# A hybrid convolution and linear-attention encoder layer in fp32: Strassen-Winograd products of halves for the projections and the final product, in a phase of their own

## The chip, the core and the metric

The kernel runs on one core of one Trainium2 chip, in one launch. The metric is the device time of one execution in microseconds (us). TensorE (PE) multiplies, VectorE (DVE), ScalarE (ACT) and GpSimd (POOL) do elementwise work, SyncE (SP) and ACT issue the DMAs that move data between DRAM and the on-chip SBUF; PE writes to PSUM, here eight banks of 128 x 512 fp32. DVE and ACT read PSUM, POOL cannot.

## The reference

Two sequences s of 1024 tokens with 1024 features go through one layer. Cut to what matters:

```
h     = rmsnorm(x) * (1 + scale) + shift                 # shift, scale, gate = silu(c) @ w_ada + b_ada
a_b, a_c, a_x, a_z, q, k, v, b_z, lr_f, lr_b, m_a, m_b = split(h @ w_in)
u     = conv3(a_c * a_x) + bias                          # along the tokens, feature by feature
y_a   = (a_b * u * silu(a_z)) @ w_a_out
g_f/b = log_sigmoid(lr_f/b @ w_gate + b_gate) / 16       # decays of the linear attention
o     = attention(q, k, v, g_f, forward) + attention(q, k, v, g_b, backward)   # 4 heads
y_b   = (rmsnorm(o) * silu(b_z)) @ w_b_out
y     = rmsnorm(x + gate * ((sigmoid(m_a) * y_a + sigmoid(m_b) * y_b) @ w_out))
```

All in fp32: eleven products of 1024 x 1024 by 1024 x 1024 for a sequence (q and k are half as wide), and the attention beside them.

## The kernel before, in words

**Products.** Every operand of a dense product is split into a rounded high part and a low rest (`split`, lines 112 to 116: an ACT cast, then a DVE or POOL subtraction), and three matmuls stand for one: high by high, high by low, low by high (`product`, lines 128 to 133). One weight tile has 128 output features; `halves` multiplies it by the activations of one sequence, which lie in SBUF as `hh` and `hl`, in two halves of 512 tokens and two steps of 12 matmuls each: 48 matmuls of 128 x 512 for a tile. The values are an exception: `values` takes the activations as the stationary operand and 256 columns of weights as the moving one, 192 matmuls of 128 x 256 for a head.

**Stages.** `start` prepares the modulation and the activations of sequence 0 and multiplies the first three weight tiles as they appear. `mixers(s)` then goes through the four heads: the projections for queries, keys, values and z gates of the head, with the decays beside them on ACT and DVE, and then `attention`. The attention of a head is a chain: seven levels of block length B = 1 to 64, where DVE multiplies Q, K and T in place, ACT rearranges K to `km`, PE multiplies 16 blocks (line 553), and DVE copies them under a mask; then transposes, states of the chunks, outputs, a norm and transposes back. Each point where it yields names a number of steps (`FILL`), and so many steps of the convolution branch (`conv_tile`, `halves`) are put there, to keep PE busy while the chain waits: 28 steps for a head of sequence 0, 32 for one of sequence 1. `merge(s)` multiplies the two branches' outputs by w_a_out and w_b_out, with the products for the merge gates between, and puts the next stationary set (the activations of sequence 1, or w_out) in place of `hh` and `hl`. `final` multiplies by w_out, 16 blocks of 128 tokens, adds x, and normalizes.

**Order and buffers.** The order on each engine is set once, at build time, by a planner: it takes the instructions by their place in the program, lets an instruction that is ready go past an earlier one that is not, and gives each tile a buffer of its tag when one is free. There are 10 `big` buffers (two rows of 1024 fp32), 8 `small` ones (one row), 2 for weights, 3 for raw loads and four PSUM banks for the dense products (`psd`). On the chip each engine takes its instructions in that fixed order.

```
def product(out, terms, first=True, last=True):
    for i, ((ahi, alo), (bhi, blo)) in enumerate(terms):
        nc.tensor.matmul(out, ahi, bhi, ...)
        nc.tensor.matmul(out, ahi, blo, ...)
        nc.tensor.matmul(out, alo, bhi, ...)
```

## Time and profile before

| what | value |
|---|---|
| median of 3 runs | 2450.72 us (2449.0 to 2453.34) |
| the profiled execution's own time | 2453.73 us |
| its span, first to last instruction | 2451.6 us |
| mean granted TensorE clock | 0.994 |
| PE, DVE, ACT, POOL busy | 98%, 49%, 35%, 9% of the span |
| instructions of PE, DVE, ACT, POOL | 12233, 1412, 1276, 171 |
| DMA | 196.24 MB, mean 80 GB/s |

The profiled execution is 3.0 us above the median of the runs; span and own time differ by 2.1 us. A matmul's duration in the rows overlaps that of its neighbours, so the pace of PE is read from the starts of successive matmuls, not from their durations.

### The profile page before, as it was taken

The numbers are of one execution on the slowest core, as the hardware profiler recorded it, in microseconds if no ns is written. First come the engines' busy times: TensorE is split into PE (matmuls) and PEld (weight loads), VectorE is DVE, ScalarE is ACT, GpSimd is POOL, SyncE is SP. The second block draws the span as 40 slices with busy tenths as digits, with TensorE's granted clock in tenths as the row PEclk, the third lists the DMA queues.
The fourth block names the chain that finished last, engine by engine and source line by source line (L and its number), as shares of the span: only waits on it lengthen the run. The fifth ranks groups of instructions, "written<-read, shape, count | busy, mean of one in ns | idle before, by whom it ended". The sixth has DMA issues, their size and how long they took to land.

```text
span 2451.6 us, 28938 instructions
## 1 busy us (share of the span) xinstructions
PE 2413.9 (98%) x12233; PEld 2037.7 (83%) x12233; DVE 1210.3 (49%) x1412; ACT 851.9 (35%) x1276; POOL 229.0 (9%) x171
## 2 busy tenths in 40 slices
PE   7999999999999999999999999999999999999998
PEld 4788888888888888888888888888888888888887
DVE  6647567567367411324466466466466411323333
ACT  5443463443433311212523523524524311212221
POOL 3101001001001000011001001001001000012421
PEclk8999999999999999999999999999999999999999
DMA  6201311311211411423201201201201411324541
GB/s 248 76 26 35 112 69 52 129 69 44 69 35 44 138 52 44 129 80 135 78 31 48 78 26 52 78 26 52 78 26 52 138 44 51 129 103 137 189 137 61
DMA packets 68322, 196.24 MB, mean 80 GB/s; under 512 B 5824, under 2 KB 22816, under 8 KB 68192
## 3 DMA queue, kind: packets, MB, share of 16 engines
q1 hardware_dynamic: 60704, 167.51, 20.2%
q10 hardware_dynamic: 7488, 26.87, 2.9%
q8 instruction: 96, 1.57, 0.3%
q14 instruction: 34, 0.28, 0.0%
HBM read 159.24 MB, written 35.13 MB: 79 GB/s over the span
## 4 chain that ended last, share of the span: by engine, by line
PE 94%; DVE 3%; issue 1%; ACT 1%; DMA 1%; POOL 0%; SPq 0%; POOLq 0%; DVEq 0%; ACTq 0%
PE ps L131 28%; PE ps L133 28%; PE ps L132 28%; PE pl L553 3%; PE pm L131 2%; PE pm L132 1%; PE pm L133 1%; PE pl L170 1%; PE ps L437 1%; PE pm L684 1%; PE pm L620 0%; DVE As L115 0%; DVE w L115 0%; PE pm L218 0%; DMA araw<-in_weights_dram 0%
## 5 line engine op out<-in xcount | busy, mean ns | idle before, releaser
L131 PE MATMUL ps<-hh,w 128*128 128x512 f32 x2032 | 801.2, 394 | 4.4 <-ACT hh L189 4.4
L133 PE MATMUL ps<-hh,w 128*128 128x512 f32 x2032 | 794.2, 391 | 0.1
L132 PE MATMUL ps<-hl,w 128*128 128x512 f32 x2032 | 794.0, 391 | 0.0
L133 PEld LDWEIGHTS ps<-hh,w 128*128 128x128 f32 x2032 | 382.5, 188 | 80.9 <-DVE w L115 0.5
L131 PEld LDWEIGHTS ps<-hh,w 128*128 128x128 f32 x2032 | 383.0, 188 | 79.6 <-ACT hh L189 4.6
L132 PEld LDWEIGHTS ps<-hl,w 128*128 128x128 f32 x2032 | 383.2, 189 | 74.7
L115 DVE TENSOR_TENSOR w<-raw,w 128x1024 fp32r<-128x1024 f32 x159 | 210.8, 1326 | 271.2 <-ACT w L114 271.2
L114 ACT CAST w<-raw 128x1024 fp32r<-128x1024 f32 x159 | 166.4, 1047 | 374.0 <-PE ps L133 359.0
L131 PE MATMUL ps<-b,w 128*128 128x512 f32 x512 | 199.2, 389 | 0.0
L132 PE MATMUL ps<-b,w 128*128 128x512 f32 x512 | 199.2, 389 | 0.0
L133 PE MATMUL ps<-b,w 128*128 128x512 f32 x512 | 199.2, 389 | 0.0
L133 PE MATMUL ps<-wv,hl 128*128 128x256 f32 x512 | 144.9, 283 | 0.0
L132 PE MATMUL ps<-wv,hh 128*128 128x256 f32 x512 | 144.9, 283 | 0.0
L131 PE MATMUL ps<-wv,hh 128*128 128x256 f32 x512 | 144.9, 283 | 0.0
L457 POOL TENSOR_TENSOR u<-u,sg 128x512 f32<-128x512 f32 x32 | 45.8, 1432 | 1047.5 <-DVE sg L456 784.3
L702 ACT ACTIVATE sg<-ps 128x512 f32<-128x512 f32 x64 | 38.3, 598 | 244.5 <-PE ps L133 244.4
L131 PEld LDWEIGHTS ps<-b,w 128*128 128x128 f32 x512 | 96.1, 188 | 20.0
L132 PEld LDWEIGHTS ps<-b,w 128*128 128x128 f32 x512 | 96.1, 188 | 20.0
L133 PEld LDWEIGHTS ps<-b,w 128*128 128x128 f32 x512 | 96.1, 188 | 19.9
L726 POOL TENSOR_TENSOR sg<-m,sg 128x512 f32<-128x512 f32 x32 | 45.0, 1405 | 657.0 <-DVE sg L725 532.2
L132 PE MATMUL ps<-hl,mg 128*128 128x512 f32 (+1 forms) x264 | 101.0, 383 | 0.0
L133 PE MATMUL ps<-hh,mg 128*128 128x512 f32 (+1 forms) x264 | 101.0, 383 | 0.0
(217 smaller groups left out, 3253.6 us busy)
## 6 DMA issues: line engine op xcount, KB each, us to landing
raw<-in_weights_dram SPq DMA_DIRECT2D x184, 512.0 KB, 3.3
araw<-in_weights_dram SPq DMA_DIRECT2D x16, 512.0 KB, 4.5
ta_d<-u ACTq DMA_DIRECT2D x16, 512.0 KB, 2.7
ob_d<-sz ACTq DMA_DIRECT2D x16, 512.0 KB, 3.8
raw<-ta_d SPq DMA_DIRECT2D x16, 512.0 KB, 4.1
raw<-ob_d SPq DMA_DIRECT2D x16, 512.0 KB, 3.5
mg_d<-sg ACTq DMA_DIRECT2D x16, 512.0 KB, 3.1
raw<-mg_d SPq DMA_DIRECT2D x16, 512.0 KB, 4.2
```

Source lines behind the costliest of these rows:

```text
L114: high = nc.scalar.copy(out=hi, in_=raw)
L115: engine.tensor_sub(out=lo, in0=raw, in1=hi.bitcast(F32))
L131: nc.tensor.matmul(out, ahi, bhi, start=(first and i == 0), stop=False)
L132: nc.tensor.matmul(out, ahi, blo, start=False, stop=False)
L133: nc.tensor.matmul(out, alo, bhi, start=False, stop=(last and i == n - 1))
L170: nc.tensor.matmul(out(t), ones if x.dtype == F32R else ones.bitcast(F32), x[:, t * HALF:(t + 1) * HALF], start=(first and i == 0), stop=( ...
L437: nc.tensor.matmul(ps[:4 * RANK], w[:, k, :], h, start=(k + i == 0), stop=(k * i == KT - 1))
L457: nc.gpsimd.tensor_mul(out=u[:, sl], in0=u[:, sl], in1=sg[:, sl])
L553: nc.tensor.matmul(pl[:, j * P:(j + 1) * P], km[:, c * P:(c + 1) * P], qm(c), start=True, stop=True)
L684: nc.tensor.transpose(out=tp[:, b * P:(b + 1) * P], in_=ot[:, b, j * P:(j + 1) * P], identity=ident)
L702: run(halves(W_MA + i, lambda ps, sl: nc.scalar.activation(out=sg[:, sl], in_=ps, func=AF.Sigmoid)))
L726: nc.gpsimd.tensor_add(out=g[:, sl], in0=m1[f][:, sl], in1=g[:, sl])
```

## The change

**The seven products.** A pair of weight tiles (256 output features, 1024 inputs) is now one job. Its weights are cut into four quarters A11, A12, A21, A22 and the activations into B11 to B22 (512 inputs by 512 tokens); seven products of quarters or of sums of quarters, in the Winograd form of Strassen's method, take the place of eight. `Moving` holds the quarters and four sums of them, `stationary` makes the seven weight operands on POOL, ACT and DVE, three products ahead of PE (`AHEAD`), and `fast` runs them in three PSUM banks a, b and c: a takes products 0 and 3, c 1 and 6, b 2, 4 and 5, with the copies and DVE additions that form the four quarters of the result between them.

**What goes through it.** The convolution's products (14 jobs of sequence 0, whose first tiles still run in `start`, 16 of sequence 1), queries, keys, values and z gates (12 jobs each), in the new phase `projections`, and the final product (8 jobs): 62 jobs. Queries, keys, values, silu(z) and the decays T go to DRAM (`q_d` to `t_d`) and are loaded again by `attention`, which transposes the values on PE. The decays run beside the q, k, v and z jobs.

**The attention's fill.** `mixers` now has only the attention, with the 64 steps of the 16 merge gates spread over heads 0 to 2 and the 32 steps of the product by w_a_out over head 3, by the lengths that `LENGTHS` gives each yield. Gates and that product go to DRAM too (`g_d`, `m1_d`); `merge` has only the product by w_b_out, beside which `refill` prepares the next `Moving`; what of it is left runs after it (`run(built)`). The `hh` and `hl` tiles are gone, and there are 18 `big` buffers, of which a `Moving` takes 16, 8 of them until the projections end.

```diff
-NBIG, NSMALL, NW, NRAW = 10, 8, 2, 3
+NBIG, NSMALL, NW, NRAW = 18, 7, 4, 3
+AHEAD = 3
+LENGTHS = (8, 5, 3, 2.5, 4, 2, 2)
+LENGTH = 8 + 7 * 5 + 2 * 3 + 4 * 2.5 + 4 * 4 + 2 * 2 + 2 * 2
...
+        def sums(self, k, x):
+            t = big("t", shape=(P, 4, HALF))
+            b11, b12, b21, b22 = (x[:, r, c * HALF:(c + 1) * HALF] for r in range(2) for c in range(2))
+            nc.gpsimd.tensor_sub(out=t[:, 0, :], in0=b12, in1=b11)
+            nc.gpsimd.tensor_sub(out=t[:, 1, :], in0=b22, in1=t[:, 0, :])
+            nc.gpsimd.tensor_sub(out=t[:, 2, :], in0=b22, in1=b12)
+            nc.gpsimd.tensor_sub(out=t[:, 3, :], in0=b21, in1=t[:, 1, :])
+            return t
+        def sum_parts(self, k, t):
+            self.th[k], self.tl[k] = big("th", F32R, (P, 4, HALF)), big("tl", F32R, (P, 4, HALF))
+            for o in range(0, 4, 2):
+                split(self.th[k][:, o:o + 2, :], self.tl[k][:, o:o + 2, :], t[:, o:o + 2, :], nc.vector)
+        def quadrant_parts(self, k, x):
+            self.hi[k], self.lo[k] = big("hi", F32R), big("lo", F32R)
+            for r in range(2):
+                split(self.hi[k][:, r, :], self.lo[k][:, r, :], x[:, r, :], nc.vector)
...
+    def stationary(load):
+        def new():
+            return sb.tile([P, 2, 4 * P], F32R, name="w", tag="w", bufs=NW)
+        def parts(a):
+            t = new()
+            split(t[:, 0, :], t[:, 1, :], a, nc.vector)
+            return t
+        r1, r2 = load(0), None
+        yield None
+        r2 = load(1)
+        r1, r2 = (r.rearrange("p k c -> p (k c)") for r in (r1, r2))
+        a11, a12, a21, a22 = r1[:, :HALF], r1[:, HALF:], r2[:, :HALF], r2[:, HALF:]
+        yield parts(a11)
+        t = new()
+        x = sb.tile([P, 4 * P], F32, name="s1", tag="s1", bufs=2)
+        nc.gpsimd.tensor_add(out=x, in0=a21, in1=a22)
+        nc.scalar.copy(out=t[:, 0, :], in_=x)
+        nc.gpsimd.tensor_sub(out=a21, in0=a11, in1=a21)
+        nc.gpsimd.tensor_sub(out=a11, in0=x, in1=a11)
+        nc.vector.tensor_sub(out=t[:, 1, :], in0=x, in1=t.bitcast(F32)[:, 0, :])
+        yield t
+        yield parts(a11)
+        yield parts(a12)
+        nc.gpsimd.tensor_sub(out=a12, in0=a12, in1=a11)
+        yield parts(a21)
+        yield parts(a22)
+        yield parts(a12)
...
+    def fast(jobs, mv):
+        ops = []
+        def make():
+            later = iter(())
+            for n, (load, _, _) in enumerate(jobs):
+                gen = later if n else stationary(load)
+                if not n:
+                    next(gen)
+                for i in range(7):
+                    if i == 2 and n + 1 < len(jobs):
+                        later = stationary(jobs[n + 1][0])
+                        next(later)
+                    ops.append(next(gen))
+                    yield
+                next(gen, None)
+        maker = make()
+        for _ in range(AHEAD):
+            next(maker, None)
+        for load, place, there in jobs:
+            banks = {}
+            for i, (o, first) in enumerate(((B11, True), (0, True), (1, True), (B21, False), (2, False), (3, False),
+                                            (B22, False))):
+                next(maker, None)
+                if first:
+                    banks["acb"[i]] = dense_ps()
+                a, b, c = (banks.get(n) for n in "abc")
+                ps = banks["acbabbc"[i]]
+                w = ops.pop(0)
+                for k in range(4):
+                    (mhi, mlo), cs = mv.operand(o, k), slice(k * P, (k + 1) * P)
+                    nc.tensor.matmul(ps, w[:, 0, cs], mhi, start=(first and k == 0), stop=False, skip_group_check=True)
+                    nc.tensor.matmul(ps, w[:, 0, cs], mlo, start=False, stop=False, skip_group_check=True)
+                    nc.tensor.matmul(ps, w[:, 1, cs], mhi, start=False, stop=(k == 3), skip_group_check=True)
+                if i == 0:
+                    keep = small("keep", shape=(P, 2, HALF))
+                    p1, u2 = keep[:, 0, :], keep[:, 1, :]
+                    nc.scalar.copy(out=p1, in_=a)
+                elif i == 2:
+                    nc.vector.tensor_add(out=u2, in0=b, in1=p1)
+                elif i == 3:
+                    nc.scalar.copy(out=place(0, 0), in_=a)
+                    there(0, 0)
+                elif i == 4:
+                    d = place(1, 1)
+                    nc.vector.tensor_add(out=d, in0=b, in1=p1)
+                    nc.vector.tensor_add(out=d, in0=c, in1=d)
+                    there(1, 1)
+                elif i == 5:
+                    nc.vector.tensor_add(out=place(1, 0), in0=b, in1=p1)
+                    there(1, 0)
+                elif i == 6:
+                    nc.vector.tensor_add(out=place(0, 1), in0=c, in1=u2)
+                    there(0, 1)
+                yield
...
+    def shift(s, f, mv, x, sl):
         by = mod[:, f, 0, s:s + 1]
-        nc.scalar.activation(out=hh[:, f, sl], in_=x, func=AF.Identity, bias=by)
-        nc.vector.scalar_tensor_tensor(out=hl[:, f, sl], in0=x, scalar=by, in1=hh.bitcast(F32)[:, f, sl],
-                                       op0=ALU.add, op1=ALU.subtract)
+        hi, lo = mv.act(f, sl)
+        nc.scalar.activation(out=hi, in_=x, func=AF.Identity, bias=by)
+        nc.vector.scalar_tensor_tensor(out=lo, in0=x, scalar=by, in1=hi.bitcast(F32), op0=ALU.add, op1=ALU.subtract)
+        nc.gpsimd.tensor_scalar(out=x, in0=x, scalar1=by, scalar2=0.0, op0=ALU.add, op1=ALU.add)
...
+    def refill(mv, src, scaled):
...
+        def load(k):
+            x = big("x")
+            nc.sync.dma_start(out=x, in_=src[k::4].rearrange("b p t -> p b t"))
+            return x
+        def prepared(k, x):
             if scaled:
-                for k, x in tiles:
-                    scale(1, k, x, rr)
-            if not half:
+                for b in range(2):
+                    scale(1, k + 4 * b, x[:, b, :], rr)
+                    nc.scalar.activation(out=x[:, b, :], in_=x[:, b, :], func=AF.Identity,
+                                         bias=mod[:, k + 4 * b, 0, 1:2])
+            return mv.sums(k, x)
+        for k in range(4):
+            x = load(k)
+            yield
+            t = prepared(k, x)
+            yield
+            if k == 2:
                 yield
-            for k, x in tiles:
-                if scaled:
-                    shift(1, k, x, slice(0, L))
-                else:
-                    split(hh[:, k, :], hl[:, k, :], x, nc.vector)
+            mv.quadrant_parts(k, x)
             yield
...
+        def conv_jobs(ct):
+            pc, px, pz, pb = tile_of("big"), tile_of("big"), tile_of("small"), tile_of("small")
+            us = {}
+            def x_there(r):
+                nc.gpsimd.tensor_mul(out=row(pc, r), in0=row(pc, r), in1=row(px, r))
+                us[r] = taps(ct + r, row(pc, r))
+            def z_there(r):
+                silu(row(pz, r), row(px, r))
+                nc.gpsimd.tensor_mul(out=us[r], in0=us[r], in1=row(pz, r))
+            def b_there(r):
+                nc.vector.tensor_mul(out=us[r], in0=us[r], in1=row(pb, r))
+                nc.scalar.dma_start(out=ta_d[s][ct + r], in_=us[r])
...
+        for h in range(0, NH, 2):
+            for w, d in ((W_Q, q_d), (W_K, k_d)):
+                jobs.append(out_job(w + h, [d[s][h + r, :, 0, :] for r in range(2)]))
+            for g in range(h, h + 2):
+                jobs.append(out_job(W_V + 2 * g, [v_d[s][g, :, r, :] for r in range(2)]))
+                jobs.append(out_job(W_BZ + 2 * g, [z_d[s][g, :, r, :] for r in range(2)], True))
+        for n, _ in enumerate(fast(jobs, mv)):
+            if n + 1 >= 7 * n_conv:
+                if n + 1 == 7 * n_conv:
+                    side = chain(prepare(), gate_rows()) if s == 0 else iter(())
+                    side = chain(decays(s, mv), side)
+                next(side, None)
+        run(side)
...
+    def mixers(s, mv):
+        def gates():
+            for i in range(2 * KT):
+                sg = small("sg")
+                yield from halves(W_MA + i, lambda ps, sl: nc.scalar.activation(out=sg[:, sl], in_=ps, func=AF.Sigmoid),
+                                  mv.act)
+                nc.scalar.dma_start(out=g_d[s][i], in_=sg)
+        def first_out():
+            act = reload(ta_d[s])
+            for f in range(KT):
+                g = small("g")
+                nc.sync.dma_start(out=g, in_=g_d[s][f])
+                yield from halves(W_A + f, lambda ps, sl: nc.vector.tensor_mul(out=g[:, sl], in0=ps, in1=g[:, sl]), act)
+                nc.scalar.dma_start(out=m1_d[s][f], in_=g)
...
-                if i % 3 == 0:
-                    next(ahead, None)
-                if i % 2 == 1:
-                    next(side, None)
-            run(ahead)
-            run(side)
-            for steps in attention(s, state, h):
-                for _ in range(steps):
+            if h == NH - 1:
+                run(dense)
+                dense, each = first_out(), KT * 4.0
+                owed = 0.0
+            for length in attention(s, h):
+                owed += each * length / LENGTH
+                while owed >= 1.0:
+                    owed -= 1.0
                     next(dense, None)
...
+    def attention(s, h):
+        n_own, n_level, n_keys, n_states, n_out, n_scale, n_turn = LENGTHS
+        T, qk = big("T"), big("qk")
+        nc.sync.dma_start(out=T, in_=t_d[s][h])
         qs, kr = qk[:, 0, :], qk[:, 1, :]
+        nc.sync.dma_start(out=qs, in_=q_d[s][h, :, 0, :])
+        nc.sync.dma_start(out=kr, in_=k_d[s][h, :, 0, :])
+        nc.scalar.mul(out=qs, in_=qs, mul=float(P) ** -0.5)
...
-        V, sz = state["V", h], state["sz", h]
+        vT, sz = big("vT"), big("sz")
+        nc.sync.dma_start(out=vT, in_=v_d[s][h])
+        nc.sync.dma_start(out=sz, in_=z_d[s][h])
+        V = big("Vh", F32R, (P, TB, DV)), big("Vl", F32R, (P, TB, DV))
+        for g in range(TB // 2):
+            tp = misc_ps()
+            for b in range(2):
+                for j in range(2):
+                    nc.tensor.transpose(out=tp[:, (2 * b + j) * P:(2 * b + j + 1) * P],
+                                        in_=vT[:, j, (2 * g + b) * P:(2 * g + b + 1) * P], identity=ident)
+            gs = slice(2 * g, 2 * g + 2)
+            split(V[0][:, gs, :], V[1][:, gs, :], tp.rearrange("p (b v) -> p b v", v=DV), nc.vector)
         Td = sb.tile([P, 2, TB], F32, name="Td", bufs=2)
         nc.vector.tensor_copy(out=Td, in_=sub_ap(T, 0, [[L, 2], [P, TB]]))
...
+    def merge(s, fill):
         act = reload(ob_d[s])
         for f in range(KT):
-            g = gates[KT + f]
+            g, m1 = small("g"), small("m1")
+            nc.sync.dma_start(out=g, in_=g_d[s][KT + f])
+            nc.sync.dma_start(out=m1, in_=m1_d[s][f])
...
-            if f == KT - 5:
-                fill = refill(src, scaled)
-            if f in (KT - 5, KT - 3, KT - 2):
-                w = load_w(W_B + f + 1)
+            next(fill)
...
+            def there(r, c):
+                sl = slice(c * HALF, (c + 1) * HALF)
+                y, x, a = place(r, c), xt[r][:, sl], ss[0][:, 2 * r + c:2 * r + c + 1]
+                (nc.vector if last else nc.gpsimd).tensor_mul(out=y, in0=y, in1=gb[s][:, sl])
+                nc.vector.tensor_add(out=y, in0=y, in1=x)
+                nc.scalar.activation(out=x, in_=y, func=AF.Square, scale=float(D) ** -0.5, accum_out=a)
+                done[r] += 1
+                if done[r] < 2:
+                    return
+                q = sb.tile([P, 1], F32, name="rs", bufs=2)
+                nc.gpsimd.tensor_scalar(out=q, in0=ss[0][:, 2 * r:2 * r + 1], scalar1=ss[0][:, 2 * r + 1:2 * r + 2],
+                                        scalar2=EPS, op0=ALU.add, op1=ALU.add)
+                nc.gpsimd.tensor_tensor(out=q, in0=q, in1=mhalf[:, :1], op=ALU.pow)
+                pieces = (((0, HALF), nc.sync), ((HALF, D), nc.scalar)) if last else (((0, D), nc.sync),)
+                for (lo, hi), queue in pieces:
+                    y = ys_[0][:, r, lo:hi]
+                    nc.vector.scalar_tensor_tensor(out=y, in0=y, scalar=q, in1=fg[:, lo:hi], op0=ALU.mult, op1=ALU.mult)
+                    queue.dma_start(out=ys[s][ts[r], lo:hi], in_=y)
...
+        run(fast([job(s, i) for s in range(2) for i in range(TB // 2)], mv))
...
+    started = start(mv)
+    projections(0, mv, started)
+    mixers(0, mv)
+    mv = Moving()
+    built = refill(mv, x_t[1], True)
+    merge(0, built)
+    run(built)
+    projections(1, mv, None)
+    mixers(1, mv)
+    mv = Moving()
+    built = refill(mv, w_out.rearrange("(k p) c -> k p c", p=P), False)
+    merge(1, built)
+    run(built)
+    final(mv)
```

## Rows read from the trace of the kernel before

**Rows 1.** The page's part 1, busy time by engine.
```profile
PE 2413.9 (98%) x12233; PEld 2037.7 (83%) x12233; DVE 1210.3 (49%) x1412; ACT 851.9 (35%) x1276; POOL 229.0 (9%) x171
```

**Rows 2.** The page's part 4, the chain that ended last, by engine.
```profile
PE 94%; DVE 3%; issue 1%; ACT 1%; DMA 1%; POOL 0%; SPq 0%; POOLq 0%; DVEq 0%; ACTq 0%
```

**Rows 3.** Timeline of PE: start, duration; one weight tile, then value products.
```profile
1120.15 0.39 PE L131 MATMUL ps<-hh,w 128*128 128x512 f32 x1
...
1131.03 0.39 PE L131 MATMUL ps<-b,w 128*128 128x512 f32 x1
...
1204.96 0.28 PE L131 MATMUL ps<-wv,hh 128*128 128x256 f32 x1
...
1216.00 0.28 PE L133 MATMUL ps<-wv,hl 128*128 128x256 f32 x1
```

**Rows 4.** The chain in order of time: transposes, then level 1 of four heads.
```profile
274.11 0.87 PE pm L684 x8
...
360.59 0.93 PE pl L170 x4
...
718.92 0.93 PE pl L170 x4
...
1255.39 0.93 PE pl L170 x4
...
1809.61 0.93 PE pl L170 x4
```

**Rows 5.** Timeline of DVE, head 1 of sequence 0 (durations in us).
```profile
378.72 1.22 DVE L594 TENSOR_TENSOR Q<-Q,t 128x1024 f32<-128x1024 f32 x1
...
388.74 1.29 DVE L597 TENSOR_TENSOR K<-K,t 128x512 f32<-128x512 f32 x2
...
405.25 0.81 DVE L471 TENSOR_SCALAR u<-pr,vecs 128x1024 f32<-128x1024 f32 x1
...
408.25 1.28 DVE L474 SCALAR_TENSOR_TENSOR u<-pr,vecs,u 128x1023 f32<-128x1023 f32 x1
```

**Rows 6.** Groups of instructions by line and shape, POOL and DVE.
```profile
L726 POOL TENSOR_TENSOR sg<-m,sg 128x512 f32<-128x512 f32 x32 | 45.0, 1405 | 657.0 <-DVE sg L725 532.2 <-issue 107.4 <-DMA raw<-mg_d 17.3
L115 POOL TENSOR_TENSOR mg<-raw,mg 128x1024 fp32r<-128x1024 f32 x16 | 40.0, 2504 | 78.3 <-ACT mg L114 78.3
L770 POOL TENSOR_TENSOR rs<-ss,consts 128x1 f32<-128x1 f32 x16 | 9.0, 564 | 1.3
L767 POOL TENSOR_SCALAR ss<-ss 128x1 f32<-128x1 f32 x17 | 5.1, 302 | 48.5 <-ACT xy L764 47.5
L725 DVE TENSOR_TENSOR sg<-ps,sg 128x512 f32<-128x512 f32 x32 | 22.0, 689 | 84.1 <-PE ps L133 83.4 <-issue 0.6
L763 DVE TENSOR_TENSOR xy<-xy 128x512 f32<-128x512 f32 x31 | 21.5, 692 | 1.1
```

**Rows 7.** Timeline of POOL and of DVE, about 410 and 423 us.
```profile
410.36 4.95 POOL L115 TENSOR_TENSOR Ql<-Q,Qh 128x2048 fp32r<-128x2048 f32 x1 [116.06 <-ACT Qh L114]
...
422.94 1.29 POOL L457 TENSOR_TENSOR u<-u,sg 128x512 f32<-128x512 f32 x1 [4.45 <-DVE sg L456]
...
410.77 4.58 DVE L604 COPY Td<-t 128x16 f32<-128x16 f32 x1
...
423.10 2.21 DVE L115 TENSOR_TENSOR w<-raw,w 128x1024 fp32r<-128x1024 f32 x1
```

**Rows 8.** Issues of DMAs on SP: KB each, median us to landing.
```profile
raw<-in_weights_dram SPq DMA_DIRECT2D x36, 512.0 KB, 3.3
...
fill<-in_x_t_dram SPq DMA_DIRECT2D x4, 1024.0 KB, 6.3
```

**Rows 9.** Two stretches: us, busy us (instructions) of PE, PEld, DVE, ACT, POOL, PEclk, DMA share, GB/s.
```profile
1226.00:1371.00 145.00, 145.00 (x758) 123.65 (x758) 92.65 (x119) 51.80 (x94) 13.40 (x9) 1.00 0.16 53
...
2248.00:2451.60 203.60, 195.79 (x887) 162.93 (x885) 76.80 (x94) 45.27 (x88) 60.16 (x53) 0.99 0.39 135
```

401 lines of the change are left out of this document (200 added, 201 removed).

## The prediction

> **What bounds the kernel now.** I read the busy times first: PE is busy for 98% of the span, DVE for half of it, POOL for 9% [rows 1]. That alone would not do, since a matmul's duration overlaps the next one's; the chain that ended last says the same from the other side, 94% of it is PE [rows 2]. So a matmul less is time less, as long as nothing else takes PE's place. The pace is in the starts: a weight tile of 48 matmuls takes 1131.03 - 1120.15 = 10.88 us, 0.2267 us for each, 2.72 us for a step of 12; the value products, 256 wide, start every 0.12 us (92 between 1204.96 and 1216.00) [rows 3]. The duration column (0.39 and 0.28) would price the same work far too high.
>
> What PE waits for today is little. Level 1 of the attention comes round every (1809.61 - 1255.39) / 3 = 184.7 us in sequence 1 and (718.92 - 360.59) / 2 = 179.2 us in sequence 0 [rows 4]. A head of sequence 1 holds 32 steps (87.0), four weight tiles for q, k and z (43.5), 192 value matmuls (23.0), four decay products (0.9), which leaves 30.3 us for the attention's own matmuls, if PE never waits there; the stretch of an attention there has PE busy all through [rows 9]. The same with 28 steps (76.2) is 173.9 us, so sequence 0 idles 5.3 us a head, 21 us in all.
>
> **The change part by part.** *Removed.* 62 jobs have 84 matmuls in place of 96: 744 x 0.2267 = 168.7 us. The values become 512 wide: 1536 x 0.12 less 768 x 0.2267 is another 10.2 us. *Added on PE.* 16 transposes of values for each of eight heads, at the 0.87 us that eight transposes take [rows 4]: 128 x 0.109 = 14.0 us. The 21 us of idle time in sequence 0 go with the arrangement that made them; what comes instead is costed below. So far: 2451.6 - 168.7 - 10.2 + 14.0 - 21 = 2266 us.
>
> *DVE and POOL in a job.* A job needs 84 x 0.2267 = 19.04 us of PE. POOL makes four sums, 128 x 512, which take 1.29 us when nothing is in the way (the row at 422.94 [rows 7]; the mean of 1.405 [rows 6] holds waits). DVE makes seven low parts of 512, 0.64 us each (half of the pair at 388.74 [rows 5]), and five additions out of PSUM, 0.69 us each [rows 6]. The convolution adds, for two feature tiles (four jobs), six POOL products of 1024 (2.5 us each [rows 6]) and on DVE two sets of taps (0.81 and twice 1.28 [rows 5]) and two products of 1.22. Neither engine alone fills the 76.2 us of four jobs: POOL 35.6, DVE 40.9.
>
> But the two are not independent. A copy of 16 elements on DVE took 4.58 us: POOL had started on Q's low part 0.4 us before; a DVE subtraction of 1.22 us took 2.21 behind a POOL operation of 1.29 [rows 7]. So I add POOL's time and DVE's operations on SBUF: 35.6 + 27.1 = 63 of 76.2 us for the convolution, which leaves PE the bound. The final job is different: POOL also multiplies the four quarters by the gate and forms the norm, 8 x 1.29 + 2 x (0.30 + 0.56) = 12.0 us, DVE has 7 x 0.64 + 4 x 0.69 + 2 x 1.28 = 9.8 us on SBUF [rows 5, 6], together 21.8 against 19.04: 2.8 us short, x 8 = 22 us.
>
> The Trainium skill, page "SBUF — State Buffer", section "Who interferes with whom", has this as an exclusive lock: a DVE instruction with two SBUF inputs and a POOL instruction that reads SBUF never run together, whichever came first holds the port to its end, and a DVE instruction with one input from PSUM is free of it. Our rows show it for POOL operations that started first. By the rule the final jobs cost the 22 us; if only each engine's own time counted, they would cost nothing, and the sum would be 22 us lower.
>
> *The new wait in a job.* Products 4 and 5 both go to bank b, and DVE must read b between them; on PE's queue every later matmul stands behind product 5. The reading is 0.69 us and some 0.3 us of signalling, if DVE is free. The cover is product 0 of the next job, 2.72 us in the fourth PSUM bank, with weights made three products ahead. Below: nothing. Above: 0.69 + 0.3 and a POOL product of 1024 ahead in the way, 3.4 us. I take 0.65 us, nearer to the lower end because the cover is longer than the reading and the two engines' shared work fills 63 of 76 us, not all. 54 jobs (the final ones are priced above) x 0.65 = 35 us.
>
> *The attention.* A head now holds 30.3 + 1.7 of its own and 64 / 3 steps (58.0): 90 us of PE; head 3 has 32 steps, 119 us. Its DVE work: the stretch of 145 us has 92.65 us [rows 9], of which about 27.5 are the convolution's and z gates' (8 weight splits of 1.22, 16 readings of PSUM of 0.69, two sets of taps); 65 remain, with the values' low parts and the gates' weight splits 74 of the 90 us. In front of each head come new loads: T, 1024 KB, 6.3 us, q and k 3.3 us each [rows 8], and most buffers for them come free only at the last chunk of the head before. SP's weight loads wait behind them, three raw tiles deep. Below: no wait, since the planner may draw later gate steps forward. Above: sequence 0 idled 5.3 us with 76.2 us of fill; 18.2 us less fill, and 6 us of loads, make 29.5 us a head. I take 7, nearer to the lower end: the fill is elastic and DVE still has 16 us to spare. Six heads: 42 us. Head 3 of either sequence must split the eight tiles of the convolution branch (8 x 1.22 on DVE) before its fill can begin: 4 us each, 8 us.
>
> *The joints.* `run(built)` leaves the last quarter of a `Moving` to be loaded and prepared after the merge: 6.3 us of load, scaling, splits and POOL sums against some 6 us of products that can start without it; before, the load was earlier in sequence 1. 10 us for both joints. In `start` POOL gets four times 5.2 us of sums: 8 us, most behind the three tiles there and `W_AB`. The merge now begins on the last head's output with no gate in front: 5 us, since three quarters of its inputs are there before. Together 23 us; nothing to 60.
>
> The extra traffic, 112 MB of writes and reads, makes some 310 MB in 2400 us, 130 GB/s; stretches of the final run at 135 today with PE almost full [rows 9]. I cost it at nothing.
>
> **Sum:** 2266 + 22 + 35 + 50 + 23 = 2396 us of span. The profiled execution's own time stands 2.1 us above its span and 3.0 above the median of the runs: 2395 us for a median.
>
> **The rivals.** *Cover throughout.* The planner fills every hole, and only the shared port of the final costs: 2266 + 22 = 2288 us. For it: PE stands at 98% today with a chain beside it [rows 1]. Against: the chip keeps the planned order whatever DVE meets.
>
> *The port decides* (slower). Place: the reading of b between products 4 and 5. If DVE comes to it behind one POOL operation and a split each time, the wait is 2.0 us, not 0.65: 54 x 1.35 = 73 us; and in the final the five PSUM additions no longer lie beside POOL, 25.3 us against 19.04, 28 more: 2396 + 101 = 2497 us. It turns the sign from about 55 / 54 us more, a wait of 1.7 us a job. For it: POOL's work grows about threefold, and every POOL operation can hold up DVE [rows 7]. Against: 13 us of 76 stay free.
>
> *The attention starves.* With the chain rigid, each of six heads waits 29.5 us: 2396 + 6 x 22.5 = 2531 us; the sign turns at 16 us a head. For it: the fill falls by a third and DVE is at 74 of 90. Against: PE never waited with DVE at 93 of 145 [rows 9].
>
> **How the numbers follow.** Forecast 0.47, cover 0.19, port 0.19, starving 0.15. A measurement of this kernel tells 0.2%, about 5 us, from no change. Faster: 0.43 of the forecast, the 0.19, and milder forms of the others 0.03: 0.65. Within: 0.02, and 0.05 of the others: 0.07. Slower: 0.28. The range takes the cover's 2290 at the one end and goes towards the port's price at the other: 2290 to 2490.
>
> **What would show it.** PE's count should be 12233 - 744 - 768 + 128 - 24 (the last block is no longer cut in three) = 10825, with starts still 0.2267 us apart. In the projections PE's idle time should be below 1 us a job, named by DVE's reading of `ps`; in the final about 3 us a job, with POOL's product by the gate ahead; in the attention of heads 0 to 2 below 10 us a head. I am wrong if PE waits 1.7 us a job or 16 us a head, or if a product of quarters is not 2.72 us long.

## The result: slower by 9.1%, and the profile after

The changed kernel takes 2675.03 us in the median (2670.13 to 2678.89), the kernel before 2450.52: a ratio of 1.0914, 95% interval 1.0893 to 1.0934. Forecast 2395, range to 2490: wrong in size and in sign.

The page of the changed kernel, parts 1 and 2 (against [rows 1]):

```profile
span 2673.8 us, 28794 instructions
PE 2377.1 (89%) x10825; PEld 1910.8 (71%) x10825; DVE 1650.0 (62%) x2033; ACT 1100.1 (41%) x1786; POOL 830.8 (31%) x525
PE   6699998887999997979999998989999997979887
PEclk8799998988999998999999999989999998989998
```

PE has the 10825 instructions that were forecast, yet its busy time fell by only 37 us and its share from 98% to 89%. The span in stretches (columns as in [rows 9]): start, convolution, q-k-v-z and attention of sequence 0, and the final product:

```profile
0.00:144.70 144.70, 96.97 (x374) 65.06 (x374) 80.80 (x96) 60.50 (x80) 94.44 (x55) 0.82 0.32 115
144.70:440.00 295.30, 275.00 (x1177) 220.74 (x1175) 175.80 (x198) 81.75 (x133) 139.24 (x77) 0.98 0.20 65
440.00:755.00 315.00, 270.64 (x1071) 208.71 (x1072) 187.41 (x215) 183.17 (x233) 81.74 (x52) 0.92 0.37 128
755.00:1205.00 450.00, 402.39 (x2184) 337.32 (x2182) 304.60 (x432) 195.40 (x380) 31.59 (x22) 0.96 0.38 140
...
2460.70:2670.00 209.30, 170.02 (x673) 133.53 (x671) 132.74 (x155) 64.75 (x137) 104.11 (x94) 0.92 0.36 118
```

In [rows 9] PE was busy for all of 145 us of attention and for 195.8 of the last 203.6 us. Now it has holes in every stretch. To count both the holes and the matmuls that ran slow I take, for every matmul, the time to the next one's start beyond its pace (0.2267 us for 512 columns, 0.12 for 256 and 128) and add it up by stretch. The kernel before lost 55.3 us in this way: 38.1 in its start, 16.1 in the heads of sequence 0, 1.0 in those of sequence 1, nothing elsewhere. The changed kernel lost 441.7. The difference, 386, less the 168.7 us saved and with the 3.8 us of other PE work, is 221 of the 224.5 us measured: the account closes, as it must, since a loss is whatever the span holds beyond the matmuls' pace. The question is what each loss is. (The sums are good to some 5 us. The start counts from the span's first instruction. The final also holds the time behind its last matmul, 7.4 us in the changed kernel and 5.6 in eight_in_phase and eight_mended; the like of it, 4.8, is not in the 55.3. Columns: kernels of the experiments below; "merge" runs from the last transposes of the attention to the first product of the next phase.)

| us lost | after | eight_in_phase | no_weight_sums | no_bank_sums | no_sums_at_all | five_mends | eight_mended |
|---|---|---|---|---|---|---|---|
| start | 77.7 | 78.2 | 79.8 | 76.5 | 79.7 | 59.6 | 40.5 |
| convolution, seq. 0 / 1 | 28.3 / 37.9 | 0 / 0 | 21.2 / 26.7 | 11.3 / 14.7 | 11.3 / 11.5 | 19.3 / 24.5 | 0 / 0 |
| q, k, v, z, seq. 0 / 1 | 69.3 / 44.6 | 17.2 / 10.7 | 57.8 / 39.9 | 66.3 / 37.1 | 55.4 / 32.4 | 35.6 / 46.5 | 1.5 / 9.6 |
| attention, seq. 0 / 1 | 43.0 / 44.2 | 41.9 / 40.7 | 44.4 / 42.4 | 45.1 / 40.3 | 42.5 / 42.6 | 48.7 / 44.1 | 44.5 / 40.7 |
| merge, seq. 0 / 1 | 19.6 / 19.6 | 24.2 / 28.2 | 19.5 / 19.8 | 19.4 / 21.2 | 19.4 / 19.5 | 1.1 / 0.6 | 0.4 / 0 |
| final | 57.5 | 5.6 | 20.6 | 56.5 | 16.3 | 35.8 | 5.6 |
| sum | 441.7 | 246.3 | 372.1 | 388.4 | 330.6 | 315.8 | 142.4 |

Where one loss comes from can be read instruction by instruction. In the final, PE's costliest group and DVE's row scale (us busy, mean ns, us of idle time before it and what ended that), then timelines of DVE, POOL and PE around one wait, and the stretch at its end (columns as in [rows 9]):

```profile
L249 PE MATMUL ps<-th,w 128*128 128x512 f32 x128 | 55.7, 437 | 30.4 <-DVE keep L257 23.5 <-ACT th L121 4.7 <-DVE y L263 2.2
...
L1013 DVE SCALAR_TENSOR_TENSOR y<-y,rs,fg 128x1024 f32<-128x1024 f32 x14 | 25.2, 1796 | 24.3 <-POOL rs L1009 24.3
```

```profile
2550.65 1.28 DVE L1013 SCALAR_TENSOR_TENSOR y<-y,rs,fg 128x1024 f32<-128x1024 f32 x1 [2.23 <-POOL rs L1009]
2551.85 1.75 DVE L122 TENSOR_TENSOR w<-raw,w 128x512 fp32r<-128x512 f32 x1
2553.53 0.68 DVE L257 TENSOR_TENSOR keep<-ps,keep 128x512 f32<-128x512 f32 x1
...
2547.90 1.67 POOL L208 TENSOR_TENSOR raw<-raw 128x512 f32<-128x512 f32 x1 [2.36 <-DVE w L122]
2549.67 0.30 POOL L1007 TENSOR_SCALAR rs<-ss 128x1 f32<-128x1 f32 x1
2550.05 0.56 POOL L1009 TENSOR_TENSOR rs<-rs,consts 128x1 f32<-128x1 f32 x1
2551.26 1.80 POOL L1000 TENSOR_TENSOR y<-y,gb 128x512 f32<-128x512 f32 x1 [0.64 <-ACT y L259]
...
2550.17 0.39 PE L251 MATMUL ps<-hi,w 128*128 128x512 f32 x1
2554.35 0.76 PE L249 MATMUL ps<-th,w 128*128 128x512 f32 x1 [3.80 <-DVE keep L257]
2554.91 0.63 PE L250 MATMUL ps<-tl,w 128*128 128x512 f32 x1
2555.34 0.63 PE L251 MATMUL ps<-th,w 128*128 128x512 f32 x1
...
2553.34:2560.17 6.83, 5.82 (x14) 4.59 (x15) 2.99 (x6) 0.97 (x3) 2.33 (x2) 0.50 0.64 197
```

Follow it back. PE stops for 3.80 us until DVE has read bank b (L257, the sum behind product 2). DVE comes late because its order has two things first. One is the row scale of a job before (L1013), which waited 2.23 us for POOL's row statistic (L1009); POOL made that behind a sum of weights (L208), which had itself waited 2.36 us for DVE (L122). The other is a low part of a weight (L122), which took 1.75 us beside POOL's product by the gate (L1000, begun 0.6 us before it), where each of the pair at 388.74 in [rows 5] took 0.64. These are small instructions, each in its place in its engine's order. And when PE comes back it is slow: the next starts are 0.56 and 0.43 us apart, not 0.2267, and the granted clock from 2553.34 to 2560.17 is 0.50, the lower of its two levels (1.2 and 2.4 GHz). In the whole trace PE has half its clock for 297 us, before the change for 34. 450 starts of 512 columns are between 0.33 and 0.5 us apart and cost 81 us; 320 of them are 0.40 to 0.45 apart, half rate, and cost 64. Before, these were 44 and 8 us, and 29 and 6. The forecast had no term for this.

### The profile page after: what moved, and what is told of

Same layout as the page of the kernel before. It is cut to its first block, busy times and chain, and to the rows that moved or that the text cites. A ratio compares the mean times of both kernels' runs of the same rounds, so it can differ in the third digit from the quotient of the medians.

```text
span 2673.8 us, 28794 instructions
## 1 busy us (share of the span) xinstructions
PE 2377.1 (89%) x10825; PEld 1910.8 (71%) x10825; DVE 1650.0 (62%) x2033; ACT 1100.1 (41%) x1786; POOL 830.8 (31%) x525
## 2 busy tenths in 40 slices
DMA packets 111724, 313.68 MB, mean 117 GB/s; under 512 B 9281, under 2 KB 42401, under 8 KB 108513
## 5 line engine op out<-in xcount | busy, mean ns | idle before, releaser
L122 DVE TENSOR_TENSOR w<-raw,w 128x512 fp32r<-128x512 f32 x506 | 441.3, 880 | 255.5 <-ACT w L121 253.8
L121 ACT CAST w<-raw 128x512 fp32r<-128x512 f32 x506 | 309.8, 619 | 590.3 <-PE ps L251 317.3
L249 PE MATMUL ps<-th,w 128*128 128x512 f32 x992 | 411.9, 416 | 80.1 <-DVE keep L257 43.5
L250 PE MATMUL ps<-tl,w 128*128 128x512 f32 x992 | 403.1, 406 | 1.0 <-DVE tl L122 1.0
L251 PE MATMUL ps<-th,w 128*128 128x512 f32 x992 | 401.8, 405 | 1.5 <-DVE w L204 0.8
L249 PE MATMUL ps<-hi,w 128*128 128x512 f32 x744 | 297.5, 400 | 24.8 <-ACT w L121 17.6
L251 PE MATMUL ps<-hi,w 128*128 128x512 f32 x744 | 294.4, 397 | 12.6 <-DVE w L122 12.6
L249 PEld LDWEIGHTS ps<-th,w 128*128 128x128 f32 x992 | 195.1, 197 | 147.4 <-issue 28.4
L250 PE MATMUL ps<-lo,w 128*128 128x512 f32 x744 | 294.6, 396 | 1.8 <-DVE lo L122 1.7
L140 PE MATMUL ps<-hi,w 128*128 128x512 f32 x560 | 228.1, 409 | 11.9 <-ACT pr L678 6.6
L251 PEld LDWEIGHTS ps<-th,w 128*128 128x128 f32 x992 | 195.6, 197 | 48.2 <-DVE w L122 3.2
L250 PEld LDWEIGHTS ps<-tl,w 128*128 128x128 f32 x992 | 196.1, 198 | 41.3 <-DVE tl L122 1.7
L141 PE MATMUL ps<-lo,w 128*128 128x512 f32 x560 | 225.6, 403 | 0.0
L142 PE MATMUL ps<-hi,w 128*128 128x512 f32 x560 | 224.9, 402 | 0.0
L249 PEld LDWEIGHTS ps<-hi,w 128*128 128x128 f32 x744 | 142.9, 192 | 62.8 <-ACT w L121 20.6
L122 POOL TENSOR_TENSOR Ql<-Q,Qh 128x2048 fp32r<-128x2048 f32 x8 | 36.9, 4611 | 462.5 <-ACT Qh L121 462.5
L208 POOL TENSOR_TENSOR raw<-raw 128x512 f32<-128x512 f32 x62 | 95.8, 1546 | 270.8 <-DVE w L122 235.9
L251 PEld LDWEIGHTS ps<-hi,w 128*128 128x128 f32 x744 | 142.1, 191 | 50.3 <-DVE w L122 20.4
```

The source lines that it names most:

```text
L121: high = nc.scalar.copy(out=hi, in_=raw)
L122: engine.tensor_sub(out=lo, in0=raw, in1=hi.bitcast(F32))
L140: nc.tensor.matmul(out, ahi, bhi, start=(first and i == 0), stop=False)
L141: nc.tensor.matmul(out, ahi, blo, start=False, stop=False)
L142: nc.tensor.matmul(out, alo, bhi, start=False, stop=(last and i == n - 1))
L208: nc.gpsimd.tensor_sub(out=a12, in0=a12, in1=a11)
```

## The experiments

Each time is the median of four runs, in brackets its ratio to before; "less" and "more" are against the changed kernel's 2675.03 us. Three theories: the **seven products** make the loss, by their sums on POOL and DVE and the port these share; the **side work** (decays, squares, gate rows, which are issued beside the products) makes it, in the engines' orders; the **joints**, where one phase hands over to the next, and the start make it.

**start_on_act.** L343: `nc.gpsimd.tensor_scalar(out=x, in0=x, scalar1=by, ...)` becomes `nc.scalar.activation(out=x, in_=x, func=AF.Identity, bias=by)`.

> Sixteen additions of the shift leave POOL (2414 ns each, 38.6 us in all) for ACT, which takes its copies from PSUM at about 0.6 us for 512 columns. If POOL's own rate sets the start: the first job of the conv phase begins 30 to 38 us earlier, POOL is busy about 56 us instead of 94 in the first 144.7 us, and the time goes from 2675 to 2637 to 2647. If the start is set by the ada weights and POOL is only one of several late engines (the waits for ACT and DVE there sum to some 15 us): 5 to 15 us, 2660 to 2670.

2656.12 us (1.0839), 19 less, between the two expectations. POOL's groups in the start of the changed kernel, then the start of this one as a stretch:

```profile
L343 POOL TENSOR_SCALAR xT<-xT,mod 128x512 f32<-128x512 f32 x16 | 38.5, 2414 | 20.3 <-DVE lo L342 20.3
L166 POOL TENSOR_TENSOR t<-xT 128x512 f32<-128x512 f32 x4 | 6.8, 1708 | 0.1
```
```profile
0.00:126.20 126.20, 92.35 (x374) 61.61 (x375) 91.33 (x96) 70.42 (x96) 61.82 (x39) 0.86 0.36 132
```

33 us off POOL took 18.5 us off the start, about half of the 39.6 that it lost more than before the change.

**eight_in_phase.** The same phases and merges, but each job is eight products of quarters, four weight parts, no additions between banks. The sums of the activations are still made, though nothing uses them:

```diff
-        a11, a12, a21, a22 = r1[:, :HALF], r1[:, HALF:], r2[:, :HALF], r2[:, HALF:]
...
+        for r in (r1, r2):
...
+            for kh in range(2):
+                yield parts(r[:, kh * HALF:(kh + 1) * HALF])
...
-            for i, (o, first) in enumerate(((B11, True), (0, True), (1, True), (B21, False), (2, False), (3, False),
-                                            (B22, False))):
+            for i in range(8):
+                r, kh, c = i // 4, i // 2 % 2, i % 2
```

> The same phases and merges, but each job is eight products of quarters: 744 matmuls more at 0.2267 us, 168.7 us of PE, no sums of weights and no additions between banks (the sums of the activations are still made, unused). If the waits in the product phases belong to the seven products (their sums on POOL, DVE's additions, three banks): the waits and slow matmuls of the conv phases and the final, some 95 us, go, and half of those beside the decays, so 2675 + 169 - 95 - 55 = 2695. If they belong to the phase itself (casts of the weights in ACT's queue, the start, the joints): 2675 + 169 - 20 = 2825.

2646.39 us (1.0799): 29 us **less** than with seven, below both expectations, though PE has 744 matmuls more. Convolution, q-k-v-z and final:

```profile
145.70:441.00 295.30, 295.30 (x1304) 244.59 (x1304) 90.07 (x111) 56.97 (x89) 48.18 (x19) 1.00 0.19 63
441.00:742.60 301.60, 289.26 (x1256) 233.79 (x1255) 140.07 (x158) 168.89 (x202) 22.79 (x9) 0.99 0.42 148
...
2462.20:2641.90 179.70, 174.24 (x769) 143.96 (x767) 84.36 (x100) 49.07 (x109) 51.70 (x61) 0.99 0.35 123
```

PE is busy for all of the convolution at full clock, and the final is 30 us shorter with 96 matmuls more. In the same surroundings seven in place of eight save 168.7 us and lose 195 (441.7 - 246.3), which is 27 of the 29 us measured. The other 2646.4 - 2450.5 = 196 us are not the new arrangement alone, since this kernel still makes the sums of the activations, which only the seven products need. eight_no_sums below leaves them out and takes 2594.5 us. So the arrangement costs 144 us, and the seven products with all their sums 81.

**b_before_c.** The product into bank b goes ahead of the one into bank c, so that b is read with two products as cover:

```diff
-        yield t
-        yield parts(a11)
+        yield parts(a11)
+        yield t
...
-            for i, (o, first) in enumerate(((B11, True), (0, True), (1, True), (B21, False), (2, False), (3, False),
+            for i, (o, first) in enumerate(((B11, True), (1, True), (0, True), (B21, False), (2, False), (3, False),
...
-                ps = banks["acbabbc"[i]]
+                ps = banks["abcabbc"[i]]
```

> Within each job the product into bank b goes ahead of the one into bank c, so the sum of bank b and p1 has two products (24 matmuls, 5.4 us) until bank b is written again instead of one (2.7 us). If DVE comes late by a fixed delay behind a queue of work (the waits are 2.7 to 2.9 us in the conv phases at every X job, 2.9 to 4.1 in the final): each of some 15 waits loses 2.7 us or all of it, 40 us, and some clock comes back: 2625 to 2640. If DVE is short of rate rather than late (busy 60 per cent there, so against it), the wait only moves to the next bank that is written again: 2665 to 2680.

2678.05 us (1.0923): no change, as its second expectation has it. PE's group in the final:

```profile
L249 PE MATMUL ps<-th,w 128*128 128x512 f32 x128 | 55.0, 431 | 27.5 <-DVE keep L257 12.0 <-ACT w L121 8.7 <-ACT th L121 4.7
```

The wait for bank b fell from 23.5 us to 12.0, and 8.7 us of waits for the weights' casts came in its place. That DVE is late by a fixed delay does not hold: PE meets the same late engines at the next thing it needs.

**side_spread** and **side_balanced.** The steps beside q, k, v and z (decays, the second sequence's squares, gate rows) advance every third product; then every second, with the gate rows in sequence 1:

```diff
-                next(side, None)
+                if (n + 1 - 7 * n_conv) % 3 == 0:
+                    next(side, None)
```

> The work beside the q, k, v and z products (decays, squares of the second sequence, gate rows) advances once every third product instead of every product, the same work in all. If PE's waits there come from ACT's and DVE's queues being filled in bursts (idle and slow matmuls 65 us in sequence 0, 45 in sequence 1, all in the part in which this work runs and none after it ended), two thirds of them go: 2675 minus 60 to 80, 2595 to 2615. If the side work costs PE a fixed wait for every one of its steps (table loads, copies), the same waits are spread thin and nothing changes: 2665 to 2680.

> The side work advances once every second product, and the gate rows move from sequence 0 to sequence 1, so that 43 and 44 steps stand beside 84 products each and one or two run bare (in the run that spread it over every third product, 26 steps ran bare: 40.6 us of waits in two places). If the bursts make the waits: sequence 0 loses 35 to 45 us, sequence 1 gains or loses up to 10: 2630 to 2645. If each step costs its own wait: 2670 to 2680.

Spread: 2660.40 us (1.0851), 15 less. Beside the products the loss fell from 69.3 to 21.3 and from 44.6 to 27.6, but in sequence 0 the 84 products took only 28 of 54 steps and the rest ran bare behind them, as PE's timeline shows:

```profile
726.96 2.55 PE L321 MATMUL pm<-sqp,ones 128*128 128x512 f32 x4 [23.29 <-ACT sqp L121]
746.83 0.80 PE L140 MATMUL ps<-hi,w 128*128 128x512 f32 x1 [17.32 <-ACT w L121]
```

Balanced: 2648.55 us (1.0809), 26 less, 26.6 of it in sequence 0; sequence 1 took the gate rows and lost the same as in the changed kernel. So what counts is how much stands beside a product. The changed kernel shows it by itself: the last decay of sequence 1 is stored at 1784.5 us, and the stretches of products before and after that are

```profile
1650.00:1795.00 145.00, 125.33 (x484) 97.10 (x483) 88.52 (x99) 127.14 (x154) 35.83 (x23) 0.91 0.34 119
1795.00:1921.00 126.00, 124.97 (x546) 101.43 (x545) 63.93 (x79) 40.30 (x64) 43.33 (x28) 1.00 0.32 110
```

With ACT at 127 of 145 us (decays, their function tables, casts) and DVE at 89, PE loses 36 us; without the decays 3. The seven products alone do not make PE wait there.

**quarters_later.** What follows a finished quarter (`there`) is issued three products later: `there(0, 0)` becomes `due.append((number + i + 3, there, (0, 0)))`, and so for each quarter.

> What is done with a finished quarter of a job (gates, taps, norm, stores) is issued three products later, so that in DVE's and POOL's order the next job's sum of bank b and p1 stands ahead of the previous job's tail. If the lateness is made by that order (in the final DVE reaches this sum 5.7 us after its bank is full, behind a row scale that waited 2.2 us for POOL): the 23.5 us of waits in the final and the 20 us in the conv phases go, with 10 to 20 us of slow matmuls: 2675 to 2620 to 2635. If POOL's and DVE's work per job is what is short (its rate, with the sums of weights): the same waits appear at another bank or at a weight part, 2665 to 2680.

2650.83 us (1.0816), 24 less, between the two expectations: in the convolution (28.3 to 18.9, 37.9 to 24.0), hardly in the final (57.5 to 54.5). DVE's order was a third of the reason in the one. That in the other the chain through POOL stays as long is likely and not shown.

**no_weight_sums, no_bank_sums, no_sums_at_all.** Parts of the computation are left out, as the expectations say: `for a in (a11, a21, a11, a12, a21, a22, a12): yield parts(a)`; one copy of a bank for each quarter; and both.

> Left out: the four sums of weight quarters of each job (56 instructions per 14 jobs, 1.33 to 1.63 us each on POOL); the seven products take plain quarters, so this part of the computation is missing, and the number of products, casts, bank additions and quarters is unchanged. If POOL's sums, and their sharing of time with DVE, hold the seven products up: the conv phases lose 20 of 28 and 25 of 38 us of waits, the final 40 of 58, q, k, v and z 20 to 40: 2675 to 2560 to 2590. If it is the order on DVE and the bank additions: conv and final unchanged, 2655 to 2675.

> Left out: the copy of p1 and the five additions from PSUM of each job; each quarter is one copy of a bank, as with eight products, so that part of the computation is missing; products, weight sums and casts stay. If the short time until a bank is written again, and DVE's six additions, make PE wait: the conv phases lose 20 of 28 and 28 of 38 us, the final 20 to 40 of 58, q, k, v and z half of 113: 2675 to 2550 to 2590. If it is the seven casts and the weight sums: conv and final lose under 10 us each, and the time is 2645 to 2670.

> Left out: both the sums of weight quarters and the additions between banks; seven products, seven casts and four copies a job stay. If the two kinds of sums are the whole difference to the eight products: conv and final at no wait as with eight, q, k, v and z at 30 to 50 us of 113, so 2675 - 66 - 52 - 70 = 2475 to 2510. If the seven casts in ACT's order beside the side work carry it: conv and final at no wait but q, k, v and z keep 80 to 113: 2525 to 2560.

2601.72 (1.0621), 2626.20 (1.0719) and 2567.95 us (1.0478): 73, 49 and 107 less, the first two between their expectations, the third 8 us above its second one. The final product of the first two:

```profile
2428.30:2601.30 173.00, 159.94 (x673) 126.38 (x671) 128.18 (x155) 65.06 (x137) 63.08 (x65) 0.97 0.44 142
```
```profile
2412.80:2621.60 208.80, 170.00 (x673) 132.81 (x671) 116.66 (x131) 62.60 (x137) 111.34 (x94) 0.93 0.34 114
```

Most of the final's loss is POOL's: 104 us of POOL there become 63, and 37 us go, while 16 us less on DVE do nothing. In the convolution it is the other way: the bank additions carry 17 and 23 us, the weight sums 7 and 11. Without either kind the seven products are 78 us faster than the eight of eight_in_phase, not 168.7: in q, k, v and z both together are worth 26 of 114, and 55 and 32 us stay. What is left there beside the side work is seven casts a job against four.

**sums_on_dve.** The four weight sums on `nc.vector` in place of `nc.gpsimd`.

> The four sums of weight quarters of each job move from POOL (1.33 to 1.63 us each) to DVE. With the sums left out the final lost 37 us, the conv phases 7 and 12. If those were POOL's time and its order (row statistics and gate products behind sums): most of it comes back here too, the final 25 to 37 us shorter, the whole 2675 minus 30 to 60, 2615 to 2645. If it was the sheer number of instructions beside the products, or DVE's own queue: DVE, which is the busiest after PE (62 per cent), comes later by about 2.7 us a job, and the time goes up, 2680 to 2740.

2681.16 us (1.0934): no gain, and both expectations came true, each in its own phase. Convolution and final:

```profile
144.50:454.40 309.90, 279.64 (x1177) 223.05 (x1176) 203.05 (x254) 81.91 (x133) 58.00 (x21) 0.97 0.19 62
...
2481.40:2672.00 190.60, 160.35 (x673) 125.97 (x671) 153.12 (x184) 64.87 (x137) 68.13 (x65) 0.98 0.39 129
```

The final is 19 us shorter, the convolution phases 15 and 17 longer: in the convolution DVE is the late one, in the final POOL.

**eight_ahead_1** and **eight_two_buffers.** Is it the lead of the weights? A part serves two products with eight, one with seven. `AHEAD = 1` in place of 3; then, since four buffers let the parts run ahead all the same, two buffers of their own for them.

> Eight products of quarters in the new phases, but each weight part is made one part (two products, 5.4 us) ahead of its use in place of three parts (16.3 us). In the seven products each part serves one product, so three parts are 8.2 us. If that lead is why the side work beside q, k, v and z costs the seven products 69 and 44 us and the eight only 17 and 11: these two phases lose 60 to 130 us in all instead of 28, and the time is 2680 to 2750. If it is the amount of casts and sums on ACT, DVE and POOL per us: the lead does not matter, 2646 to 2660.

> As eight_no_sums (2594 us; q, k, v and z lose 18.9 and 10.6 us), but the weight parts of the jobs have two buffers of their own, so a part can be ready at most one part (two products, 5.4 us) ahead; the third weight of the start and the second go into other buffers, which leaves the start's work the same. If the lead decides what the side work costs: the two q, k, v and z phases lose 60 us or more each at a median lead under 5 us, 2670 to 2720. If it is the number of casts, sums and additions per product: they lose at most 15 us more in all, 2594 to 2612, and the conv phases and the final stay without waits.

2650.67 us (1.0813) proves little, the lead having stayed. I take as lead the time from the end of a weight's low part on DVE to the first matmul that uses it, matched in order over the jobs of q, k, v and z. Its median is 13.6 and 14.8 us in the two sequences, as against 14.5 and 14.8 in eight_in_phase and 5.3 and 5.7 in the changed kernel. The two buffers brought it down to 3.6 and 3.9, and the time is 2614.54 (1.0667), 20 above eight_no_sums, q, k, v and z losing 26.1 and 21.6 us in place of 19.0 and 10.6. With eight products the lead is worth 18 us there, not the 86 that part seven from eight.

**merge_held.** `dense, each = first_out(), KT * 4.0 - 7.0`: seven steps wait until attention is over. ACT's and SP's timelines at the merge of the changed kernel, and PE's end of the wait:

```profile
1188.02 0.98 ACTq L945 DMA_DIRECT2D ob_d<-sz  x2
...
1194.62 0.32 SPq L961 DMA_DIRECT2D m<-m_d  x1
1195.87 1.54 SPq L116 DMA_DIRECT2D raw<-ob_d  x2
1197.50 0.38 SPq L116 DMA_DIRECT2D raw<-in_weights_dram  x1
...
1204.87 0.80 PE L140 MATMUL ps<-b,w 128*128 128x512 f32 x1 [17.62 <-ACT w L121]
```

> Seven of the 32 steps of the first output product (2.72 us each, 19 us) are held back until attention has ended, and stand before the second product, whose operand is on its way through DRAM then. If the 17.5 us wait at its entry is the latency of that way: 15 us per sequence go, 2675 to 2645. If attention's third of a sequence was short of cover, its own waits grow by as much: 2670 to 2680.

2642.72 us (1.0780), 32 less; the longest wait there is now 1.68 us. The last head's output is stored at 1188.0, the loads of it go out at 1195.9, and the weights behind them in SP's order: 17.6 us in which nothing else was left to multiply.

**eight_no_sums, five_mends, eight_mended.** The first is eight_in_phase without the sums of the activations. The second is the whole computation with start_on_act, quarters_later, side_balanced, merge_held and the weight sums of the final alone on DVE. The third is eight_no_sums with merge_held and the balanced side work.

> Eight products of quarters without the sums of the activations, which they do not use: no additions of the shift on POOL, no sums and casts of sums at the start and beside the merges; the computation is whole. If the longer start is all due to them: the conv phase begins at 105 to 115 us instead of 145.7, and the second merge and the final's entry lose some 10 us, 2646 to 2600. If the start is held by the ada weights, with the additions only part of it (moving them to ACT gave 19 us): 2620 to 2632.

> The whole computation with seven products, and together: the shift added by ACT (measured alone: 19 us less), quarters finished three products later (24 less), the side work every second product with the gate rows in sequence 1 (26 less), seven steps held back for the merge (32 less), and in the final alone the weight sums on DVE (the final 19 shorter where all were on DVE). If the causes are separate these add up: 2675 - 120 = 2555, within 10. If they were one shortage seen in five places, a part comes back elsewhere: 2580 to 2610.

> The whole computation with eight products in the new phases, without the unused sums (measured: 2594), with the seven held-back steps (32 us less on the seven products) and the side work every second product, gate rows in sequence 1 (the eight lose 28 us there in all, so 10 less at most): if the joints are independent of the products, 2552 to 2562. Attention's own loss, 73 us per sequence against some 43 and 27 in the stretches of the kernel before, stays, so it does not come below 2500 by any of the theories.

2594.48 (1.0583), 2546.27 (1.0390, interval 1.0375 to 1.0406) and 2540.01 us (1.0363, 1.0348 to 1.0379). The five mends add up (129 us less; 120 expected), so these were separate causes. The sums of the activations cost 52 us, 40 of them in the start (78.2 to 38.3, what it lost before the change). But seven mended products are no faster than eight, and neither is as fast as before. Of the eight's 142.4 us, 85 are attention, which before lost 17 (the 73 us a sequence of the expectation, and its 43 and 27 before, do not come out of this count). The start of eight_no_sums, and an attention stretch of eight_mended:

```profile
0.00:105.50 105.50, 83.41 (x374) 56.85 (x375) 66.61 (x88) 52.75 (x72) 30.62 (x20) 0.94 0.45 163
...
687.00:1100.90 413.90, 383.87 (x2093) 323.18 (x2092) 280.15 (x409) 186.26 (x371) 30.78 (x21) 0.96 0.34 121
```

No experiment here touched that loss. In sequence 0 of the changed kernel the longest waits named there are for the splits of transposed keys on DVE (8.4 us), and on ACT for casts (`Xh`, 7.4) and for the copy of keys to `km` (6.1); some 16 of the 43 us are in gaps under 1 us and slow matmuls.

## Why the prediction was wrong, by its own steps

**PE's own work** was right: 10825 instructions, 0.2267 us a start where nothing is late, and 168.7 us in the removed matmuls.

**The reading of bank b, 35 us** (0.65 x 54), is the step that failed most. The 54 jobs of the convolution and of q, k, v and z lost 180 us, 2.0 and 2.4 a job in the one and 5.8 and 3.7 in the other, where 1.7 was its sign of being wrong. The step argued from sums of durations, 63 of 76 us shared by DVE and POOL, and asked only for the one reading between products 4 and 5 (L263). PE's waits in the convolution and in the q, k, v and z of sequence 0:

```profile
L249 PE MATMUL ps<-th,w 128*128 128x512 f32 x224 | 90.7, 405 | 8.9 <-DVE keep L257 8.1 <-DVE pair L263 0.9
...
L249 PE MATMUL ps<-th,w 128*128 128x512 f32 x192 | 81.2, 423 | 18.6 <-ACT w L201 6.9 <-DVE single L263 6.3 <-ACT w L121 4.2
...
L249 PE MATMUL ps<-hi,w 128*128 128x512 f32 x144 | 59.1, 411 | 14.3 <-ACT w L121 11.9 <-ACT keep L255 2.4
...
L732 PE MATMUL ps<-hi,wlr 128*64 128x512 f32 x16 | 7.6, 476 | 11.1 <-DVE wlr L122 11.1
```

The planner did put four matmuls into that place in the convolution, and over both sequences PE waited 13 us for that reading. It waited 20 us for the sum behind product 2 (L257), which has only product 3 as cover until product 4 writes bank b again, 45 for weights (their casts, low parts and sums), and 22 for the decays' own operands. Some 35 of the 180 are matmuls at half clock. Each engine takes its instructions in order, and a chain such as the one in the final runs through three of them: shares of 60% did not mean being in time.

**The port in the final, 22 us**, had the right place and engine, and the sign that it gave, about 3 us a job: the seven waits for bank b are 3.4 us on average. But the final's matmuls lost 50 us (57.5 with the end), of which POOL's weight sums cost 37. The sum of durations was set against 19.04 us a job, without the chain that a row statistic makes between POOL and DVE, which waited 24.3 us for it, and without the slow matmuls behind each wait. The lock of the Trainium skill's "SBUF — State Buffer" ("Who interferes with whom") fits what is seen: the sums on POOL took 1.33 to 1.63 us in the convolution, against 1.29 alone [rows 7], and the low part of 1.75 us above stood beside a POOL product. It doesn't give the time by itself: with the sums off POOL the final gained and the convolution lost.

**Attention, 50 us less the 21 of sequence 0**, was right in kind: 87 us lost against 17 before, so 70 and not 29.

**The joints, 23 us**, were 79. The start lost 39.6 us more, where the step counted POOL's four sets of sums (8 us) and overlooked sixteen additions of 2.41 us. The two merges lost 39.2, priced at 5, since "three quarters of its inputs are there" says nothing of SP's order, in which the weights stood behind the last quarter. The 10 us for the last quarter of a `Moving` did not come: with that wait filled, the merges of five_mends lost 1.1 and 0.6.

**Left out altogether:** the side work beside q, k, v and z, which costs even the eight products 28 us; and the clock, some 60 us more at half rate than before, contained in the losses above.

**The rivals.** "Cover throughout" did not hold. "The port decides" had the sign and, in the final, the mechanism, but its place for the other 54 jobs (products 4 and 5) was the wrong one. "Attention starves" came about at half its price and was not what decided. (The upper bound of a job's reading, 0.69 + 0.3 + 2.5 us, is 3.5 and not 3.4, which changes nothing.)

**Open:** why attention loses 43 us per sequence, since no run gave it more steps to fill its waits or fewer loads; how the 88 us left in q, k, v and z without any sums divide between the three further casts and their order, the lead having been tried only with eight products; and what the traffic costs, which came as forecast (313.68 MB) and was varied by no run.

## What to carry to other kernels

A matmul saved is time saved only if what feeds and drains it can be late without PE noticing: count, for every bank and buffer, how long PE can go on, and compare that with the longest chain through the engines' orders, not with their busy shares. Work that is merged into long phases of one kind can lose the cover that the mixture gave it: in eight_no_sums attention and the merges lose 107 us more than before. Try the arrangement without the cheaper arithmetic, and without what only that arithmetic needs, first: here that one run, eight_no_sums, showed 144 of the 225 us.

## What was not expected of the hardware

A POOL addition of a per-partition scalar with a second scalar operation took 2414 ns for 128x512, POOL's tensor additions and subtractions beside it 1275 to 1708 ns in the mean. After short waits the granted clock fell: it is 0.92 in the final, with waits of some 3.4 us a job for bank b, and 0.99 in that of eight_in_phase, where next to nothing waits. So a wait cost again in slow matmuls. And ACT's change of function tables is not small: the decays alone make 32 in one q-k-v-z phase, four lines like this one, 41 us of its 315:

```profile
L765 ACT ACT_TABLE_LOAD x8 | 10.3, 1283 | 0.5 <-issue 0.4
```

The Trainium skill's "ScalarE: Activation LUTs" ("What ACT_TABLE_LOAD costs") gives the same 1283 ns for the load and about 1380 more for a drain, some 2.7 us for a change of set. In this trace only the load shows: one starts at 458.73 us and the next activation at 460.03. The section "Table sets: the hidden batching unit" of that page of the Trainium skill has a set that holds both exp and ln, with which the decays' loads would be fewer; no run here tried it.
